# A hybrid decoder layer on one core: arithmetic moved off GpSimd at the start, rotary tables put behind the row factors, four accumulating DMAs a pass later, small tiles of 64 bytes

## The chip, the cores and the metric

The kernel runs on one core of a Trainium2 chip, in one launch. The metric is the device time in microseconds (us). Before the change three runs gave a median of 783.87 us (783.56 to 784.42).

The core has these engines: TensorE (PE in the profile; its weight loads are PEld), VectorE (DVE), ScalarE (ACT), GpSimd (POOL) and SyncE (SP), which only issues DMAs. Each runs its own queue of instructions in a fixed order and waits on semaphores for the others. VectorE, ScalarE and GpSimd work on SBUF; TensorE writes its results to PSUM.

## The reference

One decoder layer on 512 tokens of width 1024, in float32. In short:

```python
u = rms_norm(x, norm_mix_g)
proj = u @ w_in          # conv a and g (512 + 512), c_q (384), c_kv (256), k_rope (32), gates (2 x 1024)
z = a * sigmoid(g); z = depthwise_causal_conv(z, conv_w, width=31) + conv_b
conv_out = silu(layer_norm(z)) @ w_conv_out
mla_out  = latent_attention(c_q, c_kv, k_rope, cos, sin) @ w_mla_out     # 8 heads, causal
h = x + (sigmoid(g0) * conv_out + sigmoid(g1) * mla_out) @ w_out
h = h + memory_cross_attention(rms_norm(h, norm_xattn_g), rms_norm(mem, norm_mem_g))   # 4 heads, 256 memory tokens
h = h + square(relu(rms_norm(h, norm_mlp_g) @ w_mlp1)) @ w_mlp2          # 4096 wide
y = rms_norm(h, final_norm_g)
```

## The kernel before

Every product of two float32 matrices is done with three matmuls on rounded halves: a matrix is split into hi (a cast to the matmul type on ScalarE, L202) and lo (a subtract, L203, on VectorE or GpSimd), and `mm3` (L237 to L239) adds hi·hi, hi·lo and lo·hi into one PSUM bank. The weights come in chunks of 1 MB from HBM into two `raw` buffers through SyncE's queue. `prep` splits a chunk's part into one of three `wh`/`wl` pairs, and `w_eng[0]` says which engine does the subtract. `Pipe` splits one unit ahead of the matmuls that use it.

The order of TensorE's instructions is the program's. `after(ticks, fn)` puts a small piece of work some steps of `mm3` later into that order. The queues of the other engines are ordered by a scheduler when the program is built: it takes what is ready first by its own model of time, and of several ready ones the one that comes first in the program. On the chip that order is fixed.

The first stage (L608 to L641) computes the projection onto the conv channels, in four channel tiles of an a and a g half each. For channel tile 0 the transfers of `x` and of the weights still arrive; per block of 128 rows of `x`, `split_x` makes `uh` and `ul` (L206, L207), and the weight block is split, its lo part on GpSimd from block 1 on. `x_stats` squares x and adds up the eight squares, three adds on VectorE and four on GpSimd (L579, L580). For channel tile 1 the weights' lo is made on VectorE, from channel tile 2 on by GpSimd. After the a half of tile 1 `x_rows` sums the squares over the rows with eight small matmuls (L277) and computes the row factors `rx` on VectorE (L279, L245 to L250), then `rx2`, its square (L584). Five steps later `x_bcast` transposes `rx` (L271), copies it to `rbx` and evacuates the g half of tile 0 with it (`evac_g`, L600 to L605); then it makes the tables of the rotary angles (`rope_tables`, L439 to L462: four multiplies at L444, one per token tile, and some twenty steps on 128x64), which depend on constants and positions alone. The sines themselves are ScalarE's (L467, L468). The conv taps (L492, L494: 31 per channel tile on VectorE) begin as soon as a tile's gate is ready, and are spread over the projections that follow.

The memory branch keeps its row factors in `rm`, 2 values per row, in the pool `xm`; the pools `mg` (`mgh`, `mgl`: the merged branches) and `x2` are stacked on it. `xm` also holds the split memory (`mh`, `ml`), its keys and its values (`xvh`, `xvl`).

The last stage is the second MLP matrix in seven passes over sums of blocks (`PASSES`, L1384; four units `c` each), which replaces eight products of blocks by seven. Its weight operands are sums of the four blocks b11, b12, b21 and b22. They are formed in place: `add_to` (L1356) issues a DMA from GpSimd that adds a block of `w_mlp2` from HBM to a tile in SBUF. The tiles `xs[c]` start as b11 (`load_x`, SyncE's queue). Each of the passes 0, 2 and 4 reads `xs[c]` and then adds the next block, for the pass two later; pass 3 does the same with `vs[c]`. Pass 1 reads `b21[c]`, loaded in passes 0 and 1 by `load_b21` into tiles that other blocks have left; `load_v` loads b22 in pass 2. Two of the blocks of the hidden layer (s3, a22) are spilled to HBM and read back by `reload` from ScalarE's queue.

Of the kernel before, what the change touches and what calls it, by code (L numbers as in the profile page):

```python
# [14 lines left out]
F32 = mybir.dt.float32  # L15
# [4 lines left out]
ALU = mybir.AluOpType  # L20
# [3 lines left out]
P = 128  # L24
# [144 lines left out]
def _body(tc, a):  # L169
# [3 lines left out]
    dve = nc.vector  # L173
    act = nc.scalar
    gps = nc.gpsimd

    def pool(name, bufs=1, side=None, space=None):
        kw = dict(name=name, bufs=bufs, reuse_waits="tile")
        if side:
            kw["side"] = side  # L180
        if space:
            kw["space"] = space
        cm = tc.tile_pool(**kw)
        return cm, cm.__enter__()
# [5 lines left out]
    cst_cm, cst = pool("cst")  # L190
# [10 lines left out]
    def split(hi, lo, src, eng=None):  # L201
        act.copy(hi, src)  # L202
        (eng or dve).tensor_tensor(lo, src, hi.bitcast(F32), op=ALU.subtract)  # L203
# [38 lines left out]
    def rsqrt(dst, v, n):  # L242
        t = sm.tile([P, n], F32, tag="rs_t", name="rs_t")
        ti = sm.tile([P, n], I32, tag="rs_i", name="rs_i")
        dve.tensor_scalar(ti, v.bitcast(I32), 1, None, op0=ALU.logical_shift_right)  # L245
        dve.tensor_scalar(dst.bitcast(I32), ti, -1, 0x5F3759DF, op0=ALU.mult, op1=ALU.add)
        for _ in range(3):
            dve.scalar_tensor_tensor(t, dst, -0.5, dst, op0=ALU.mult, op1=ALU.mult)  # L248
            dve.tensor_tensor(t, t, v, op=ALU.mult)
            dve.scalar_tensor_tensor(dst, t, 1.5, dst, op0=ALU.add, op1=ALU.mult)  # L250
# [10 lines left out]
    rx = cst.tile([P, NT], F32, name="rx")  # L261
    rx2 = cst.tile([P, NT], F32, name="rx2")
# [31 lines left out]
    raws = {}  # L294
# [37 lines left out]
    w_eng = [dve]  # L332
# [32 lines left out]
    xr = xp.tile([P, KD, S], F32, name="xr")  # L365
    nacc = xp.tile([P, S], F32, name="nacc")
# [62 lines left out]
    def split_x(k):  # L429
        split_scaled(uh[:, k, :], ul[:, k, :], xr[:, k, :], v_("norm_mix_g", k))  # L430


    n = NT * 16
# [5 lines left out]
    def rope_tables():  # L439
        dve.tensor_copy(posf, posi)  # L440
        fr = kon[:, K_FREQ:K_FREQ + n]
        for t in range(NT):
            sl = slice(16 * t, 16 * t + 16)
            dve.tensor_scalar(ang[:, sl], fr[:, sl], posf[:, t:t + 1], None, op0=ALU.mult)  # L444

        def fma(k, c):
            dve.scalar_tensor_tensor(ang, k, -c, ang, op0=ALU.mult, op1=ALU.add)

        dve.tensor_scalar(k_, ang, 1.0 / TWO_PI, MAGIC, op0=ALU.mult, op1=ALU.add)
        dve.tensor_scalar(k_, k_, MAGIC, None, op0=ALU.subtract)  # L450
        dve.tensor_scalar(kh, k_, 2.0 ** -11, MAGIC, op0=ALU.mult, op1=ALU.add)
        dve.tensor_scalar(kh, kh, MAGIC, 2048.0, op0=ALU.subtract, op1=ALU.mult)
        dve.tensor_tensor(k_, k_, kh, op=ALU.subtract)
        for c in PI_PARTS:
            fma(kh, c)
            fma(k_, c)
        dve.tensor_scalar(k_, ang, 1.0 / TWO_PI, MAGIC, op0=ALU.mult, op1=ALU.add)
        dve.tensor_scalar(k_, k_, MAGIC, None, op0=ALU.subtract)
        for c in PI_PARTS:
            fma(k_, c)  # L460
        dve.tensor_scalar(ang, ang, 3.1415925, -3.1415925, op0=ALU.min, op1=ALU.max)
        dve.scalar_tensor_tensor(k_, ang, -1.0, ang, op0=ALU.mult, op1=ALU.max)  # L462
# [109 lines left out]

    hold = {}

    def x_stats():
        for k in range(KD):
            act.activation(xr[:, k, :], xr[:, k, :], AF.Square)
            if k > 1:
                (dve, gps)[k % 2].tensor_tensor(xr[:, k % 2, :], xr[:, k % 2, :], xr[:, k, :], op=ALU.add)  # L579
        gps.tensor_tensor(nacc, xr[:, 0, :], xr[:, 1, :], op=ALU.add)  # L580

    def x_rows():
        rstd_rows(nacc, D, rx)
        dve.tensor_tensor(rx2, rx, rx, op=ALU.mult)  # L584

    def x_bcast():
        b = bcast_rows(rx)
        act.copy(rbx, b)
        hold["a"] = fa
        evac_g(fg, 0)  # L590
        act.copy(identb, ident)
        act.copy(maskb, kon[:, K_MASK:K_MASK + 128])
        rope_tables()


    def evac_a(b, c):
        hold["a"] = b
# [12 lines left out]
    for k in range(KD):  # L610
        hl = first[k // 4]
        if k == 0:
            dve.tensor_copy(hl[0][:, 0], raws[0][:, 0])
            dve.tensor_tensor(hl[1][:, 0], raws[0][:, 0], hl[0][:, 0].bitcast(F32), op=ALU.subtract)
        split_x(k)
        if k == 1 or k > 0 and k % 2 == 0:
            kn = 1 if k == 1 else 2
            sl = slice(k % 4, k % 4 + kn)
            split(hl[0][:, sl], hl[1][:, sl], raws[0][:, k:k + kn], gps)
        for i, j in ((0, 0), (1, 0), (0, 1)):  # L620
            for b, c0 in ((fa, 0), (fg, 128)):
                pe.matmul(b, hl[i][:, k % 4, c0:c0 + 128], (uh, ul)[j][:, k, :],
                          start=k == 0 and i == j == 0, stop=k == KD - 1 and j == 1)
        tick(2.0)
# [10 lines left out]
        evac_g(b, 1)  # L635

    for c in range(1, CT):
        w_eng[0] = dve if c == 1 else gps
        proj_unit(("ag", c), 0, evac_a1 if c == 1 else lambda b, c=c: evac_a(b, c))
        proj_unit(("ag", c), 128, evac_g1 if c == 1 else lambda b, c=c: evac_g(b, c))  # L640
    pipe.flush()  # L641
# [195 lines left out]
    for t in range(NT):  # L837
        b = bank()
        sl = slice(t * P, (t + 1) * P)
# [56 lines left out]
    xm_cm, xmp = pool("xm", side="right")  # L896
# [4 lines left out]
    mh = xmp.tile([P, KD, MEM], F32R, name="mh")  # L901
    ml = xmp.tile([P, KD, MEM], F32R, name="ml")
    rbm = xmp.tile([P, MEM], F32, name="rbm")
    rm = xmp.tile([P, 2], F32, name="rm")
    mg_cm, mgp = pool("mg", side="right")
    mgh = mgp.tile([P, KD, S], F32R, name="mgh")
    mgl = mgp.tile([P, KD, S], F32R, name="mgl")
# [32 lines left out]
    def mem_norm():  # L940
        ms = sm.tile([P, 2], F32, tag="mss", name="mss", bufs=1)
        for t in range(2):
            act.activation(mtok[:, t, :], mtok[:, t, :], AF.Square, accum_out=ms[:, t:t + 1])
        v = sm.tile([P, 2], F32, tag="rv2", name="rv2", bufs=1)
        dve.tensor_scalar(v, ms, 1.0 / D, EPS, op0=ALU.mult, op1=ALU.add)
        rsqrt(rm, v, 2)
        for k in range(KD):
            split_scaled(mh[:, k, :], ml[:, k, :], mr[:, k, :], v_("norm_mem_g", k))
        after(D_M, mem_bcast)
# [260 lines left out]
    xs, vs = {}, {}  # L1210
# [145 lines left out]
    def add_to(t, what, c):  # L1356
        gps.dma_start(out=t, in_=hbm(what, c), accum_op=ALU.add, max_dma_last_dim=8192)  # L1357

    def w_source(n, c):

        if n in (0, 2, 4, 6):
            return xs[c], {0: "b12", 2: "b22", 4: "b21"}.get(n)
        if n in (3, 5):
            return vs[c], {3: "b12"}.get(n)
        return b21[c], None

    b21 = {}
# [94 lines left out]
    def pass_unit(n, c):  # L1462
        aname, bk, again = PASSES[n]
        end = n == len(PASSES) - 1

        def prep_():
            if aname in SPILLED:
                for cc in {0: (0, 1), 3: ()}.get(c, (c + 1,)):
                    reload(aname, cc)
            src, nxt = w_source(n, c)  # L1470
            h, w = split_h(aname, c), split_w(v3(src))
            if n == 0 and c >= 2:
                load_b21(c - 2)
            if n == 1 and c < 2:
                load_b21(2 + c)
            if n == 2:
                load_v(c)
            if nxt:
                add_to(src, nxt, c)
            return h, w  # L1480

        def main(hw):
            h, w = hw
            if c == 0 and not again:
                acc_[bk] = [bank("at" if bk in "bd" else "mm") for _ in range(2)]
            if end and c == 2:
                held["hw"] = hw
            elif end and c == 3:
                for t in range(2):
                    part(acc_[bk][t], t, *held["hw"], False, False, again)  # L1490
                    part(acc_[bk][t], t, h, w, False, True, again)
                    DONE[n](t)
            elif c in (0, 3):
                for t in range(2):
                    part(acc_[bk][t], t, h, w, c == 0 and not again, c == 3, again)
                    if c == 3:
                        DONE[n](t)
            else:
                chunk(acc_[bk], h, w, c, again)
            if n == 0 and c == 0:  # L1500
                late_pools()
                load_x(3)
            if n == 2 and c == 0:
                m2w["gf"] = w_tile(m2w["p"], "b21", "gf")[:, :D]
                dma(out=m2w["gf"], in_=a["gfin"].to_broadcast([P, D]))
        pipe.unit(prep_, main)
# [32 lines left out]
```

## Time and profile before

| what | value |
|---|---|
| median of 3 runs | 783.87 us |
| profiled execution, its time | 785.28 us |
| its span, first to last instruction | 783.5 us |
| mean granted clock of TensorE | 0.991 |
| PE busy | 757.7 us (97%), 3594 matmuls |
| PEld busy | 626.3 us (80%) |
| DVE busy | 526.9 us (67%) |
| ACT busy | 400.3 us (51%) |
| POOL busy | 91.2 us (12%), 70 instructions |
| DMA | 103.36 MB, 132 GB/s over the span |

Busy time is the time in which an engine has an instruction at work; matmuls overlap their neighbours, so the mean of one (389 ns) is longer than the time from one start to the next. [...] In lists in order of time the number in brackets is the engine's idle time ahead of the row, and behind the arrow stands what ended it. "POOLq", "SPq" and "ACTq" are the queues that issue DMAs.

### The profile page before, as it was taken

What the parts mean: (1) busy time and instruction counts of PE and PEld (TensorE: products, weight loads), DVE (VectorE), ACT (ScalarE), POOL (GpSimd) and SP (SyncE); (2) the same over time, 40 slices, a digit from 0 to 9 for tenths busy, and PEclk for the clock granted to TensorE, in tenths of its full rate; (3) what the DMA queues carried; (4) which work ended last, traced back from release to release, by engine and by line L of the source; (5) the groups of instructions that cost most, each with busy time, mean ns of one, the idle gap of its engine ahead of it and who ended that gap; (6) DMA issues with size and microseconds to landing.
All of it is one profiled execution on the core that took longest, in us unless ns stands there. A gap on an engine that the chain in (4) does not pass through costs nothing.

```text
span 783.5 us, 9480 instructions
## 1 busy us (share of the span) xinstructions
PE 757.7 (97%) x3594; PEld 626.3 (80%) x3594; DVE 526.9 (67%) x845; ACT 400.3 (51%) x681; POOL 91.2 (12%) x70
## 2 busy tenths in 40 slices
PE   8799999999999999999999999999999979999996
PEld 4589789778788887889888888888888868888784
DVE  5898999944788869756687634333333546767995
ACT  7422244378766647434474644444444445665662
POOL 4434436330000000000000000000000000111000
PEclk9899999999999999999999999999999999999998
DMA  8313223312203134424231424334253696999731
GB/s 277 106 40 108 84 85 108 107 54 95 94 1 108 55 108 161 161 63 154 108 108 54 162 92 164 135 132 179 106 215 109 184 277 239 246 231 214 192 108 54
DMA packets 26990, 103.36 MB, mean 132 GB/s; under 512 B 2369, under 2 KB 9921, under 8 KB 17985
## 3 DMA queue, kind: packets, MB, share of 16 engines
q1 hardware_dynamic: 13600, 67.54, 24.1%
q0 software_dynamic: 2304, 16.78, 10.5%
q10 hardware_dynamic: 11040, 18.45, 6.8%
q8 instruction: 28, 0.46, 0.3%
q14 instruction: 18, 0.14, 0.1%
HBM read 94.37 MB, written 8.39 MB: 131 GB/s over the span
## 4 chain that ended last, share of the span: by engine, by line
PE 79%; DVE 13%; DMA 3%; ACT 2%; issue 2%; SPq 0%; DVEq 0%; ACTq 0%
PE mm L239 20%; PE mm L237 20%; PE mm L238 20%; DVE cv L494 6%; PE at L238 4%; PE at L239 4%; PE at L237 4%; DMA a<-weights 2%; PE at L812 1%; PE at L793 1%; DVE wl L203 1%; DMA xr<-xT 1%; DVE rs_t L248 1%; DVE sg L721 1%; PE at L794 1%
## 5 line engine op out<-in xcount | busy, mean ns | idle before, releaser
L202 ACT CAST wh<-raw 128x1024 fp32r<-128x1024 f32 (+4 forms) x103 | 102.6, 998 | 193.0 <-PE mm L238 165.5
L203 DVE TENSOR_TENSOR wl<-raw,wh 128x1024 fp32r<-128x1024 f32 (+1 forms) x71 | 85.7, 1207 | 105.7 <-ACT wh L202 105.5
L237 PE MATMUL mm<-hgh,wh 128*128 128x512 f32 x288 | 113.2, 393 | 0.0
L238 PE MATMUL mm<-hgl,wh 128*128 128x512 f32 x288 | 112.2, 389 | 0.0
L239 PE MATMUL mm<-hgh,wl 128*128 128x512 f32 x288 | 112.2, 389 | 0.0
L494 DVE SCALAR_TENSOR_TENSOR cv<-zpad,vec,cv 128x512 f32<-128x512 f32 x116 | 80.0, 743 | 0.1
L203 POOL TENSOR_TENSOR wl<-raw,wh 128x1024 fp32r<-128x1024 f32 (+4 forms) x32 | 66.1, 2066 | 96.7 <-ACT wh L202 96.7
L237 PE MATMUL mm<-uh,wh 128*128 128x512 f32 x176 | 71.0, 404 | 2.3 <-DVE sg L721 2.1
L1357 POOL DMA_DIRECT2D x<-weights x12 | 10.5, 879 | 516.1 <-DVE wl L203 496.1
L239 PE MATMUL mm<-uh,wl 128*128 128x512 f32 x176 | 69.7, 396 | 0.5 <-DVE wl L203 0.5
L238 PE MATMUL mm<-ul,wh 128*128 128x512 f32 x176 | 69.6, 395 | 0.0
L239 PEld LDWEIGHTS mm<-hgh,wl 128*128 128x128 f32 x288 | 54.1, 188 | 11.4
L237 PEld LDWEIGHTS mm<-hgh,wh 128*128 128x128 f32 x288 | 54.1, 188 | 10.9
L238 PEld LDWEIGHTS mm<-hgl,wh 128*128 128x128 f32 x288 | 54.1, 188 | 10.9
L203 DVE TENSOR_TENSOR wl<-x,wh 128x1024 fp32r<-128x1024 f32 x25 | 30.3, 1220 | 18.9 <-ACT wh L202 18.9
L237 PEld LDWEIGHTS mm<-uh,wh 128*128 128x128 f32 x176 | 33.8, 192 | 10.7 <-issue 4.2
L239 PEld LDWEIGHTS mm<-uh,wl 128*128 128x128 f32 x176 | 33.6, 191 | 8.3 <-DVE wl L203 1.0
L238 PEld LDWEIGHTS mm<-ul,wh 128*128 128x128 f32 x176 | 33.7, 192 | 6.6
L202 ACT CAST wh<-x 128x1024 fp32r<-128x1024 f32 x25 | 26.2, 1051 | 24.4 <-PE at L239 9.7
L238 PE MATMUL at<-wl,hA 128*128 128x512 f32 x96 | 37.6, 391 | 0.6 <-DVE wl L203 0.6
L239 PE MATMUL at<-wh,hB 128*128 128x512 f32 x96 | 37.4, 389 | 0.0
L237 PE MATMUL at<-wh,hA 128*128 128x512 f32 x96 | 37.4, 389 | 0.0
(392 smaller groups left out, 1721.2 us busy)
## 6 DMA issues: line engine op xcount, KB each, us to landing
raw<-weights SPq DMA_DIRECT2D x42, 1024.0 KB, 4.9
x<-weights POOLq DMA_DIRECT2D x12, 1024.0 KB, 11.6
a<-weights SPq DMA_DIRECT2D x5, 1024.0 KB, 9.1
x<-weights SPq DMA_DIRECT2D x4, 1024.0 KB, 6.0
raw<-weights SPq DMA_DIRECT2D x4, 768.0 KB, 4.3
xr<-xT SPq DMA_DIRECT2D x8, 256.0 KB, 6.1
raw<-weights SPq DMA_DIRECT2D x4, 512.0 KB, 5.0
ht<-xT ACTq DMA_DIRECT2D x1, 2048.0 KB, 9.1
```

The source lines that it names most:

```text
L202: act.copy(hi, src)
L203: (eng or dve).tensor_tensor(lo, src, hi.bitcast(F32), op=ALU.subtract)
L237: pe.matmul(out, wh, ah, start=first and i == 0, stop=False, **kw)
L238: pe.matmul(out, wh, al, start=False, stop=False, **kw)
L239: pe.matmul(out, wl, ah, start=False, stop=last and i == n - 1, **kw)
L248: dve.scalar_tensor_tensor(t, dst, -0.5, dst, op0=ALU.mult, op1=ALU.mult)
L494: dve.scalar_tensor_tensor(run if w < CW - 1 else acc[:, c, :], zs, wcol, run, op0=ALU.mult, op1=ALU.add)
L721: dve.tensor_tensor(t, b, rbx, op=ALU.mult)
L793: pe.matmul(b[:, :n], q[:, 0, sl], k[:, 1, :n], start=False, stop=False)
L794: pe.matmul(b[:, :n], q[:, 1, sl], k[:, 0, :n], start=False, stop=True)
L812: pe.transpose(b[:, (t - k) * P:(t - k + 1) * P], ptok[h, t][:, k * P:(k + 1) * P], ident)
L1357: gps.dma_start(out=t, in_=hbm(what, c), accum_op=ALU.add, max_dma_last_dim=8192)
```

## The change

Five edits:

- The lo part of channel tile 0's weights, the adds of `x_stats` and the lo parts of channel tile 2's weights are done by VectorE. From channel tile 3 on GpSimd does them as before.
- VectorE's instructions of `rope_tables` are queued behind the one that writes `rx2`. `tc.issue_after(ins)` orders what its block issues on the engine of `ins` behind `ins`; it adds no wait.
- The four DMAs that add b12 to `xs[c]` are issued in pass 1 instead of pass 0, each behind a copy on GpSimd (`pace`) of one column of the first lo weights of pass 1's unit c. Pass 2 reads the sums, as before.
- `rm` has 16 columns (64 bytes in each partition) instead of 2.
- The new tile `paced` has 16 columns as well, in the pool of constants at the left.

```diff
+    rx_done = []
     def x_stats():
         for k in range(KD):
             act.activation(xr[:, k, :], xr[:, k, :], AF.Square)
             if k > 1:
-                (dve, gps)[k % 2].tensor_tensor(xr[:, k % 2, :], xr[:, k % 2, :], xr[:, k, :], op=ALU.add)
-        gps.tensor_tensor(nacc, xr[:, 0, :], xr[:, 1, :], op=ALU.add)
+                dve.tensor_tensor(xr[:, k % 2, :], xr[:, k % 2, :], xr[:, k, :], op=ALU.add)
+        dve.tensor_tensor(nacc, xr[:, 0, :], xr[:, 1, :], op=ALU.add)
     def x_rows():
         rstd_rows(nacc, D, rx)
-        dve.tensor_tensor(rx2, rx, rx, op=ALU.mult)
+        rx_done.append(dve.tensor_tensor(rx2, rx, rx, op=ALU.mult).ins)
...
-        rope_tables()
+        with tc.issue_after(rx_done[0]):
+            rope_tables()
...
-            split(hl[0][:, sl], hl[1][:, sl], raws[0][:, k:k + kn], gps)
+            split(hl[0][:, sl], hl[1][:, sl], raws[0][:, k:k + kn])
...
-        w_eng[0] = dve if c == 1 else gps
+        w_eng[0] = dve if c < 3 else gps
...
-    rm = xmp.tile([P, 2], F32, name="rm")
+    rm = xmp.tile([P, 16], F32, name="rm")
...
-        rsqrt(rm, v, 2)
+        rsqrt(rm[:, :2], v, 2)
...
+    paced = cst.tile([P, 16], F32, name="paced")
+    def pace(lo):
+        return gps.tensor_copy(paced[:, 0:1], lo[:, 0, 0:1].bitcast(F32)).ins
     def w_source(n, c):
         if n in (0, 2, 4, 6):
-            return xs[c], {0: "b12", 2: "b22", 4: "b21"}.get(n)
+            return xs[c], {2: "b22", 4: "b21"}.get(n)
...
             if nxt:
                 add_to(src, nxt, c)
+            if n == 1:
+                with tc.issue_after(pace(w[0][1])):
+                    add_to(xs[c], "b12", c)
```

## Rows read from the trace of the kernel before

**Rows 1.** Order of time, TensorE: start, duration, line, tiles; last, idle time and releaser
```profile
26.23 0.95 PE L277 MATMUL at<-ones,nacc 128*128 128x1 f32 x8
...
35.64 1.09 PE L271 MATMUL at<-kon,rx 128*128 128x128 f32 x4 [4.89 <-issue]
...
41.22 0.63 PE L239 MATMUL mm<-uh,wl 128*128 128x512 f32 x1
...
645.16 0.50 PE L237 MATMUL mm<-wh,hA 128*128 128x512 f32 x1 [4.33 <-ACT s L1389]
...
743.09 0.50 PE L238 MATMUL at<-wl,hA 128*128 128x512 f32 x1 [0.61 <-DVE wl L203]
```

**Rows 2.** Order of time, VectorE, first 70 us
```profile
13.43 5.84 DVE L207 SCALAR_TENSOR_TENSOR ul<-xr,vec,uh 128x512 fp32r<-128x512 f32 x4
...
19.20 0.68 DVE L579 TENSOR_TENSOR xr<-xr 128x512 f32<-128x512 f32 x1
19.80 1.21 DVE L203 TENSOR_TENSOR wl<-raw,wh 128x1024 fp32r<-128x1024 f32 x1
...
25.06 4.88 DVE L444 TENSOR_SCALAR ang<-kon,posf 128x16 f32<-128x16 f32 x4
29.98 0.20 DVE L449 TENSOR_SCALAR k__164<-ang 128x64 f32<-128x64 f32 x1
...
32.93 0.15 DVE L279 TENSOR_SCALAR rv<-at 128x4 f32<-128x4 f32 x1
...
68.66 1.90 DVE L603 TENSOR_TENSOR sg<-sg,rbx 128x512 f32<-128x512 f32 x1 [3.17 <-ACT sg L602]
```

**Rows 3.** Order of time, GpSimd: two subtracts, and one of the accumulating DMAs
```profile
24.96 4.82 POOL L203 TENSOR_TENSOR wl<-raw,wh 128x1024 fp32r<-128x1024 f32 x2
...
630.53 0.88 POOL L1357 DMA_DIRECT2D x<-weights  x1 [1.66 <-DVE wl L203]
```

**Rows 4.** By tile, TensorE: count, ns minimum/median/maximum, first and last start, shape
```profile
L238 PE MATMUL mm<-mgl,wh x64: 395/396/504, 308.6 to 353.4; 128*128 128x512 f32 x64
...
L238 PE MATMUL mm<-hgl,wh x288: 387/389/398, 366.4 to 615.4; 128*128 128x512 f32 x144
...
L238 PE MATMUL mm<-ul,wh x176: 387/389/628, 20.1 to 191.4; 128*128 128x512 f32 x176
...
L237 PE MATMUL at<-wh,hA x96: 388/389/395, 687.7 to 773.9; 128*128 128x512 f32 x96
```

**Rows 5.** Stretches: busy us of PE, PEld, DVE, ACT, POOL, clock, DMA share, GB/s
```profile
30.00:42.00 12.00, 7.11 (x22) 5.47 (x21) 7.10 (x35) 3.78 (x7) 0.00 (x0) 0.72 0.18 66
68.00:146.00 78.00, 75.61 (x392) 65.58 (x390) 77.34 (x124) 27.91 (x53) 36.53 (x25) 1.00 0.28 97
640.80:650.00 9.20, 4.87 (x15) 3.86 (x15) 4.81 (x4) 4.89 (x6) 0.00 (x0) 0.81 1.00 282
654.00:666.00 12.00, 12.00 (x55) 9.93 (x54) 7.61 (x8) 6.46 (x8) 0.86 (x1) 1.00 0.47 162
666.00:733.00 67.00, 67.00 (x297) 55.49 (x296) 48.23 (x46) 40.39 (x45) 9.53 (x11) 1.00 1.02 229
```

**Rows 6.** Chain of waits in order of time, 620 to 650: start, us, what
```profile
629.06 13.47 DMA a<-weights
```

**Rows 7.** DMA issues, us to landing: windows 600 to 612, 629.5 to 636, 727 to 730
```profile
x<-weights SPq DMA_DIRECT2D x1, 1024.0 KB, 5.0
...
x<-weights POOLq DMA_DIRECT2D x1, 1024.0 KB, 21.4
...
re_s<-s ACTq DMA_DIRECT2D x1, 512.0 KB, 7.6
```

**Rows 8.** Page, part 3, queues: packets, MB, share of 16 engines over the span
```profile
q1 hardware_dynamic: 13600, 67.54, 24.1%
q0 software_dynamic: 2304, 16.78, 10.5%
```

**Rows 9.** Order of time, ScalarE: the cast of the reloaded block
```profile
736.62 1.06 ACT L202 CAST hA<-re_s 128x1024 fp32r<-128x1024 f32 x1 [0.23 <-PE at L238]
```

## The prediction

> **What bounds the kernel now.** I read the busy shares first, then TensorE in order of time at its two long gaps, then what VectorE, GpSimd and the transfers did before each. TensorE is busy 757.7 of 783.5 us. What can be won lies in its 25.8 idle us, in the slow clock behind the gaps, and in matmuls that take longer than others.
>
> First gap: TensorE stands 4.89 us until the transposes of L271 at 35.64 [rows 1]. They need rx, so VectorE is late: its row factors start at 32.93 only [rows 2], though the sums that they read (L277) were through at 27.2 [rows 1]. In between stand the rotary tables, and these were slow: four multiplies of 128x16 took 4.88 us while GpSimd ran two subtracts, 24.96 to 29.78 [rows 2, 3]; the next table step, 128x64, took 0.20. [...]
>
> From 68 to 146 VectorE is busy 77.34 of 78 us, TensorE 75.61 [rows 5]: both nearly full. VectorE's last slack before that is 3.17 us ahead of L603 at 68.66, where it waits for ScalarE [rows 2].
>
> Second gap: 4.33 us before 645.16, clock 0.81 in the 9.2 us from 640.8 [rows 1, 5]. The chain of waits names a load of b21 of 13.47 us [rows 6]; the same size took 5.0 us while no accumulating DMA was out [rows 7]. The four of pass 0 are: the last is issued at 630.53 and lands 21.4 us later, near 652 [rows 3, 7].
>
> **The change, part by part.** The sum is made against the profiled execution (span 783.5, time 785.28: 1.78 us lie outside the span). The median of the runs, 783.87, is 1.41 below it.
>
> *GpSimd's work to VectorE.* VectorE takes over a subtract of 128x256 (some 0.4, from the 0.68 of a 512-wide add), three of 128x512 (0.68), four adds (three squares and nacc, 0.68) and the two subtracts of channel tile 2 (1.21): 0.4 + 2.0 + 2.7 + 2.4 = 7.5 us [rows 2]. Given back: four L207 took 5.84 from 13.43, at 0.68 they are 2.7, so 3.1 less; the four table multiplies at 0.20 are 0.8 for 4.88, so 4.1 less [rows 2]. Net 0.3 more: VectorE is about as full as before, but the 3.1 come off the first 20 us, where TensorE waits for ul. Bounds there: 0 (x's transfers set the pace) and 3.1. I take 1.5, the middle: neither row is nearer.
>
> *Tables behind the row factors.* Only VectorE's order changes. With TensorE 1.5 us earlier the sums are through at 25.7. The factors are twelve small steps; between 32.93 and 35.6, with table steps among them, they took 2.7. One 1.21 us subtract may stand in front. So rx is there by 29.6, and L271 comes up at 30.75 - 1.5 = 29.25. I drop the 0.35: the 4.89 us go, and with the gap its slow clock, 6.0 us of work at half rate (35.64 to 41.6), 3.0 lost. Together 7.9; bounds 5 (1.21 us more in front, slow clock half kept) and 7.9. What is late next: the tables, some 27 steps of 0.2, 5.4 us, now run from 29.5 among the first gate evacuations, and the conv taps of L494 queue behind both, perhaps 2 us less ahead than TensorE. The 3.17 us at 68.66 cover that, because the wait there hangs through ScalarE on TensorE [rows 2]; without this cover each us is paid in full in the stretch to 146. The two sines on ScalarE wait for the tables, and nothing waits for them before the key rotation, some 100 us on. Front: 1.5 + 7.9 = 9.4.
>
> *Small tiles of 64 bytes.* In the layout a tile of 8 bytes takes 32. So rm puts its pool and those stacked on it (xkh, mh, xvh, mgh and their halves) 32 bytes off the place within 64 bytes that all other large tiles share. The matmuls show a difference: median 396 ns with mgl against 389 with hgl, ul and hA, all 512 wide [rows 4]. 192 matmuls with mgh or mgl, 48 with mh or ml, 24 with xvh or xvl: 264 x 7 ns = 1.8 us, TensorE being full there. Bounds 0 and 1.8; I take 1.8, since three neighbours agree on 389. The tile paced, 64 bytes, moves everything on the left by 64, which keeps that place; rival C doubts it. [...]
>
> *Accumulating DMAs one pass on.* Nothing is then beside the load of b21 at 629.06, so it takes 5.0 instead of 13.47 [rows 6, 7] and lands near 634, before its cast is due at some 638. The 4.33 go, and the slow clock: 0.19 x 2 x 9.2 = 3.5 us at half rate, of which some 3.2 with work, 1.6 lost. Together 5.9. Each moved step issues a one-column copy on GpSimd (0.20, the small VectorE step, or three times that) and the DMA (0.88 [rows 3]). The copy waits for the first wl of its unit in pass 1. Behind it on GpSimd stand only the next such steps, and no engine waits for GpSimd there. SP's loads (b21, v, gf) have their own queue and share only the DMA engines. Due times, an estimate from the pace of the units, 24 matmuls at 67 us for 297, so 5.4 us [rows 5]: issue near 633.5, 639.5, 644.5, 648.5; pass 2 reads the four tiles some 18 to 20 us later. Landing: 5.0 for such bytes alone, 21.4 at worst [rows 7]; issued 5 us apart instead of 2.5, I take 12 to 15: in time.
>
> Given back: the sixteen accumulating DMAs cost 10.5% of 783.5, 82.3 us of all engines, 5.1 each; a plain MB costs 2.8 (24.1% for 67.54 MB) [rows 8]. From 666 to 733 the engines are full at 1.02 [rows 5]. In the place that pass 0's four leave (20.6 us) some 5 MB of other transfers fit, 14 us; so 6.5 us of engine time are lost there. Free later on are 12 x 0.53 = 6.4, between 654 and 666 [rows 5]. So the sixteenth lands when it did, within 1 us. Behind it comes the reload of s3's third block: it took 7.6 us and was cast at 736.62, for the unit whose second matmul starts at 743.09 [rows 1, 7, 9]. Of these 6.5 us the cast is 1.06 and the matmul ahead some 1, so 4.4 are slack. TensorE wants the reload 5.9 earlier, it comes 1 earlier: 4.9 - 4.4 = 0.5 us late. Bounds 0 and 5.9. Net 5.4.
>
> Sum: 9.4 + 1.8 + 5.4 = 16.6. Span 766.9, that execution 768.7, median **767.3 us**.
>
> **The rivals.**
> A. *VectorE becomes the bound of the first 68 us.* The 7.5 us come without the relief (if it was not GpSimd that slowed those steps). Less 3.17 of slack, 4.3 are lost: 771.6. For it: VectorE is full up to 146. Against: the multiplies end just as GpSimd does, and the next step takes 0.20 [rows 2, 3].
> B. *The wait only moves.* The DMA engines stay the bound, and the reload of pass 5, or pass 2's tiles, come late by what was won: 5.4 lost, 772.7. For it: 67 us at 1.02, landings of 21.4. Against: the 6.4 free us ahead of pass 2. [...]
> C. *Slower.* What costs the 7 ns is the place not in 64 bytes but in 128, and paced moves every left tile, wh and wl among them, off the good one. Then the wide matmuls pay: 288 + 176 + 96 on each of three lines [rows 4] are 1680, and 750 of the page's other matmuls (3594 in all) lie on the same weights: 2430 x 7 ns = 17.0, and the 1.8 are not won: 786.1. It decides from 2340 on. For it: no large tile of before lies at the new place. Against: 7 ns are about 16 of the 512 columns that pass in 226 ns, 64 bytes.
> D. *The tables do not let go.* Splits stand ahead of the factors, and half of the 4.89 stays, without the slow clock: 769.8.
>
> **How the numbers follow.** Forecast 0.60, A 0.14, B 0.13, C 0.05, D 0.05, no net effect 0.03. The forecast's own ends: 1.6 more in the first 20 us and some 2 of the 2.4 idle us of 68 to 146 [rows 5] saved besides give 763.5; 2.9 less at the tables gives 770.2. A, B and D reach to 772.7; with a us on each side 763 to 774. Faster by over 0.2% (1.6 us, about what a measurement tells from none): forecast, A, B and D, 0.92. Within it 0.03. Slower, C, 0.05.
>
> **What would show it.** Right: no gap over 1 us before L271, clock 1.00 from 25 to 45 and from 630 to 650; table multiplies near 0.2 us, L207 below 0.8; mgl at 389 ns; the b21 load under 7 us; pass 1's DMAs landing within 16. Wrong: TensorE waiting for VectorE between 30 and 68 (A), for re_s or for x in pass 2 (B), 396 ns with hgl (C), rx still behind splits (D).

## The result and the profile after

The changed kernel takes 774.56 us, median of four runs (774.36 to 775.09), against 784.14 of the kernel before beside them: ratio 0.988 (95% interval 0.986 to 0.990). The forecast was 767.3 with a range of 763 to 774, so the direction was right, the gain of 16.6 us came out at 9.6 to 10.2, and the time lies half a us above the range. The profiled execution took 775.09 us, span 773.2.

I matched the matmuls of both traces one by one in program order and read how far TensorE runs ahead of the kernel before (times of before in brackets): 9.4 us at the end of the first projection (41.7), 7.1 at 262, 7.1 at 640, 13.2 at 665, 12.4 at 742, 10.6 at 745, 10.4 at the end. Two steps up, as forecast; between them two slow slides and one step down.

The front. In order of time on TensorE, in the changed kernel, the row sums, the transposes that had waited 4.89 us [rows 1], and a matmul late in pass 5:

```profile
24.54 0.95 PE L277 MATMUL at<-ones,nacc 128*128 128x1 f32 x8
...
28.98 0.62 PE L271 MATMUL at<-kon,rx 128*128 128x128 f32 x4
...
732.50 0.50 PE L238 MATMUL at<-wl,hA 128*128 128x512 f32 x1 [2.42 <-DVE wl L203]
```

L271 has no idle time ahead of it now. The last row had 0.61 before [rows 1] and has 2.42. VectorE in order of time:

```profile
15.51 1.41 DVE L207 SCALAR_TENSOR_TENSOR ul<-xr,vec,uh 128x512 fp32r<-128x512 f32 x2
...
25.53 0.16 DVE L279 TENSOR_SCALAR rv<-at 128x4 f32<-128x4 f32 x1 [2.19 <-PE at L277]
...
26.41 1.22 DVE L203 TENSOR_TENSOR wl<-raw,wh 128x1024 fp32r<-128x1024 f32 x1
...
28.91 0.16 DVE L586 TENSOR_TENSOR rx<-rx 128x4 f32<-128x4 f32 x1
...
29.19 0.65 DVE L444 TENSOR_SCALAR ang<-kon,posf 128x16 f32<-128x16 f32 x4
```

Two of L207 take 1.41 us where four took 5.84, four of L444 take 0.65 where they took 4.88 [rows 2], and the row factors run from 25.53 to 29.07 with one subtract of 1.22 among them.

The stretches of [rows 5] in the changed kernel (same columns; its own times):

```profile
30.00:42.00 12.00, 12.00 (x53) 9.64 (x52) 11.86 (x26) 4.64 (x6) 4.43 (x2) 1.00 0.07 30
...
640.80:650.00 9.20, 9.20 (x42) 7.55 (x41) 6.05 (x6) 5.05 (x5) 1.07 (x2) 1.00 1.04 252
654.00:666.00 12.00, 12.00 (x54) 9.87 (x53) 9.06 (x9) 7.67 (x9) 1.72 (x2) 1.00 1.03 275
```

The granted clock, a share of TensorE's full speed, is 1.00 where it was 0.72 and 0.81, TensorE has no idle time there, and the transfer engines are full from 654 to 666, where before they had half of the time free.

The slide. Two stretches that hold the same 1122 matmuls, first the kernel before, then the changed one:

```profile
42.00:266.00 224.00, 219.83 (x1122) 185.39 (x1121) 187.66 (x339) 117.89 (x231) 59.03 (x35) 1.00 0.23 78
```

```profile
32.56:258.90 226.34, 223.07 (x1122) 185.35 (x1121) 191.91 (x351) 120.81 (x236) 58.99 (x35) 1.00 0.22 77
```

2.34 us longer, and TensorE does not stand more (3.3 us idle against 4.2): it is busy 3.2 us longer with the same work. By tile, TensorE, as in [rows 4]:

```profile
L238 PE MATMUL mm<-mgl,wh x64: 387/393/506, 301.6 to 346.3; 128*128 128x512 f32 x64
...
L238 PE MATMUL mm<-hgl,wh x288: 387/389/397, 359.3 to 608.4; 128*128 128x512 f32 x144
...
L238 PE MATMUL mm<-ul,wh x176: 388/394/399, 18.8 to 183.6; 128*128 128x512 f32 x176
...
L237 PE MATMUL at<-wh,hA x96: 388/392/398, 674.7 to 763.5; 128*128 128x512 f32 x96
```

`ul` went from 389 to 394 ns and `hA` from 389 to 392, `hgl` stayed, and `mgl` came from 396 to 393 only. From start to start the medians are 227 ns where nothing is lost and 233 for `uh` and `ul`.

The step down. The chain of waits of the changed kernel in pass 5 (start, us, what):

```profile
713.18 1.06 ACT hA L202
714.25 1.24 DVE hB L203
715.51 11.30 DMA re_s<-s
726.89 1.06 ACT hA L202
727.98 1.23 DVE hB L203
...
730.57 0.74 DVE y L1406
731.31 1.15 DVE wl L203
732.50 0.50 PE at L238
```

The reload of s3's third block can be issued only when VectorE has made the lo half of the first one (they share a buffer), and takes 11.30 us instead of 7.6 [rows 7].

### The profile page after: what moved, and what is told of

Its sections match the earlier page's. It is cut to its first block, busy times and chain, and to the rows that moved or that the text cites. A ratio compares the mean times of both kernels' runs of the same rounds, so it can differ in the third digit from the quotient of the medians.

```text
span 773.2 us, 9487 instructions
## 1 busy us (share of the span) xinstructions
PE 756.4 (98%) x3594; PEld 623.8 (81%) x3594; DVE 525.3 (68%) x855; ACT 399.9 (52%) x681; POOL 76.4 (10%) x64
## 4 chain that ended last, share of the span: by engine, by line
PE 80%; DVE 13%; DMA 3%; ACT 2%; issue 1%; SPq 0%; DVEq 0%; ACTq 0%
PE mm L239 21%; PE mm L238 21%; PE mm L237 21%; DVE cv L494 6%; PE at L238 4%; PE at L237 3%; PE at L239 3%; DMA re_s<-s 1%; PE at L816 1%; DVE wl L203 1%; PE at L797 1%; DVE rs_t L248 1%; DMA xr<-xT 1%; PE at L798 1%; PE at L795 1%
## 5 line engine op out<-in xcount | busy, mean ns | idle before, releaser
L203 DVE TENSOR_TENSOR wl<-raw,wh 128x1024 fp32r<-128x1024 f32 (+3 forms) x77 | 90.7, 1178 | 106.7 <-ACT wh L202 106.4
L494 DVE SCALAR_TENSOR_TENSOR cv<-zpad,vec,cv 128x512 f32<-128x512 f32 x116 | 80.4, 744 | 0.1
L203 POOL TENSOR_TENSOR wl<-raw,wh 128x1024 fp32r<-128x1024 f32 (+2 forms) x26 | 56.4, 2169 | 107.7 <-ACT wh L202 102.9
L237 PEld LDWEIGHTS mm<-hgh,wh 128*128 128x128 f32 x288 | 54.1, 188 | 10.9
L238 PEld LDWEIGHTS mm<-hgl,wh 128*128 128x128 f32 x288 | 54.1, 188 | 10.9
L1368 POOL COPY paced<-wl 128x1 f32<-128x1 f32 x4 | 2.5, 615 | 468.2 <-DVE wl L203 468.2
```

The costliest lines, as they stand in the source:

```text
L237: pe.matmul(out, wh, ah, start=first and i == 0, stop=False, **kw)
L238: pe.matmul(out, wh, al, start=False, stop=False, **kw)
L494: dve.scalar_tensor_tensor(run if w < CW - 1 else acc[:, c, :], zs, wcol, run, op0=ALU.mult, op1=ALU.add)
L1368: return gps.tensor_copy(paced[:, 0:1], lo[:, 0, 0:1].bitcast(F32)).ins
```

## Experiments

Two theories stood at the start. *Places*: what sets a matmul's cadence is where its two operands lie against each other, and `paced` moved one of them. *Traffic*: the matmuls are slower because of what VectorE or the transfers do beside them.

**left_back.** `paced` is gone; rm stays at 64 bytes.

```diff
-    paced = cst.tile([P, 16], F32, name="paced")
-        return gps.tensor_copy(paced[:, 0:1], lo[:, 0, 0:1].bitcast(F32)).ins
+        return gps.tensor_copy(posi[:, 0:1].bitcast(F32), lo[:, 0, 0:1].bitcast(F32)).ins
```

> The changed kernel without the tile paced: the copy of one column goes into posi, a tile of constants that nobody reads by then, so that wh, wl and all other left tiles lie where they lay before the change. rm keeps its 64 bytes. Theory 1 (the place of the stationary tile against the moving one sets the cadence): matmuls of uh and ul with wh go from 233 back to 227 ns from start to start, those of hA from 229 to 232 back to 227, cq, ck and pt likewise; TensorE's lead on the kernel before stays near 9.4 us up to 266 us instead of falling to 7.1. 3.2 us less than the changed kernel's 774.6: 771.4. mgh and mgl stay slow (232 or more), since they lie at another place than wh. Rival (the cadence comes from other traffic, say VectorE's larger share of the splits or the later DMAs): uh stays at 233 and the time at 774.6 +- 0.6.

Measured: 771.84 (771.06 to 772.68), ratio 0.983 (0.982 to 0.985) to before's 784.84. By tile:

```profile
L238 PE MATMUL mm<-ul,wh x176: 387/389/397, 19.2 to 182.3; 128*128 128x512 f32 x176
...
L238 PE MATMUL mm<-mgl,wh x64: 392/394/505, 299.5 to 344.5; 128*128 128x512 f32 x64
```

`ul` is back at 389, the lead stays at 9.1 up to 262 and at 16.2 through the passes, and `mgl` is still slow. 64 bytes among the constants cost some 3 us.

**all_same.** The same, with the tiles on rm's pool at wh's place too.

```diff
-    rm = xmp.tile([P, 16], F32, name="rm")
+    rm = xmp.tile([P, 128], F32, name="rm")
```

> As left_back, and rm has 128 columns (512 bytes), so that the tiles stacked on its pool (mh, xvh, mgh and their halves) lie at the same place within 512 bytes as wh and uh. Theory 1: 227 ns with mgh and mgl too; 264 matmuls by 5 to 7 ns are 1.3 to 1.8 us less than left_back, 769.9 (769.4 to 770.4). Rival: the same as left_back and the changed kernel; or, if 232 to 235 ns with mgl come from what else happens at that stage and not from the place, left_back's time with uh at 227 and mgl at 232.

Measured: 771.33 (770.11 to 773.03), ratio 0.983 (0.981 to 0.984).

```profile
L238 PE MATMUL mm<-mgl,wh x64: 389/389/504, 298.7 to 342.6; 128*128 128x512 f32 x64
```

`mgl` is at 389, and the stretch from 262 to 355 gives 1.0 us. The median lies 1.4 above the 769.9 that was expected; it is only 0.5 better than left_back's and the ranges overlap. In the stage behind, where `mh`'s matmuls are 256 columns wide, all_same runs about 0.6 us behind left_back (120 ns from start to start against 113; there the two operands lie at the same place modulo 256 bytes in all_same and 192 apart in left_back). Why 256 columns behave otherwise was not followed.

**shift_alone.** The kernel before with the 64 bytes alone.

```diff
+    paced = cst.tile([P, 16], F32, name="paced")
+    gps.memset(paced, 0.0)
```

> The kernel before with nothing but the tile paced, 64 bytes among the left constants, and one memset that writes it. Theory 1: uh and ul with wh go from 227 to 233, hA from 227 to 229 to 232, hgh stays at 227, since hgh and wh move together; about 3 us slower than before, 787.2 (786.5 to 788). Rival (other traffic): 784.1 +- 0.5, uh at 227. The rival of the prediction in its full size, 7 ns on some 2400 matmuls, would be 801.

Measured: 788.00 (787.53 to 789.95), ratio 1.0044 (1.0029 to 1.0058): 3.4 us slower by the ratio, for a tile that nothing reads.

```profile
L238 PE MATMUL mm<-ul,wh x176: 388/394/628, 20.6 to 193.0; 128*128 128x512 f32 x176
...
L237 PE MATMUL at<-wh,hA x96: 388/397/398, 690.9 to 778.5; 128*128 128x512 f32 x96
```

**shift_256.** As shift_alone, with `[P, 64]`, 256 bytes.

> As shift_alone, with the tile paced of 64 columns, 256 bytes, instead of 16. Theory 1 (the cadence depends on the difference of the two operands' addresses modulo 256 bytes): uh, ul and hA back at 227 ns, mgl at 235 as before, time as before, 784.7 +- 0.6. [...]

Measured: 784.73 (783.22 to 786.14) beside 784.66, ratio 1.0002 (0.9991 to 1.0013).

```profile
L238 PE MATMUL mm<-ul,wh x176: 387/389/628, 20.5 to 190.3; 128*128 128x512 f32 x176
```

**places.** The cadence by itself.

```diff
+        b, g = go(0, 32)   # stationary 0, moving 32 bytes off; one such pair of lines per place
+        for s, m, f, l in g: pe.matmul(b, s, m, start=f, stop=l)
```

> It leaves out the whole computation: 68 groups of 24 matmuls of 512 columns, each group on its own line, with the stationary operand 0, 96 or 224 bytes off a place and the moving one 0 to 480 bytes off it in steps of 32; then eight places again while ScalarE and VectorE run splits of 128x1024, and again while loads of 1 MB arrive. Theory 1: a group has 227 ns from start to start where both places are the same, and some 230 to 236 where they differ, in the quiet part already; which differences cost tells the modulus (64, 128, 256 or 512 bytes). Rival: 227 in every quiet group; if the place matters only beside other engines, the second or third part shows it, and if it never does, what slowed uh was not the place.

Measured in one run, groups by line (last but one number: mean ns of one). The moving operand is 32 (L207), 128 (L213), 64 (L209), 256 (L221) and 0 bytes (L205) past the stationary one; L283 has both at 224:

```profile
L207 PE MATMUL bk<-mv,st 128*128 128x512 f32 x24 | 5.8, 395 | 0.0
...
L213 PE MATMUL bk<-mv,st 128*128 128x512 f32 x24 | 5.8, 395 | 0.0
...
L209 PE MATMUL bk<-mv,st 128*128 128x512 f32 x24 | 5.7, 392 | 0.0
...
L221 PE MATMUL bk<-mv,st 128*128 128x512 f32 x24 | 5.6, 390 | 0.0
...
L283 PE MATMUL bk<-mv,st 128*128 128x512 f32 x24 | 5.6, 390 | 0.0
...
L205 PE MATMUL bk<-mv,st 128*128 128x512 f32 x24 | 5.6, 389 | 0.0
```

What counts there is the difference (moving minus stationary) modulo 256 bytes, over the 48 quiet groups at multiples of 32. At 0 a matmul is 389 to 390 ns, 227 from start to start; at 64 it is 391 to 392 (229); at the others it is 394 to 396 (233 to 234). Four more groups, at 4, 16, 48 and 80 bytes, have 393 to 399. It shows with no other engine at work, and the parts with splits and with loads have the same numbers (392 at 64, 390 at 256). The kernel's own pairs fit (addresses modulo 256 in the built programs: before, all of these at 224 but mgl at 192; after, wh at 32, mgl at 160, uh, ul and hA at 224): in the changed kernel `uh` and `ul` lie 192 past `wh` (233.5), `mgl` 128 past it (232), `wh` 64 past `hA` (229.0 over its three lines); in the kernel before `mgl` lay 224 past it (233.3). One thing stays open: in shift_alone `wh` lies at the same 64 past `hA` and the passes run at 233, steadily, up to pass 5; those of the changed kernel run at 229. So the same pair of places settled in two rhythms here, and what chose was not found.

**move_alone.** The kernel before with the four DMAs in pass 1, no tile moved.

```diff
-            return xs[c], {0: "b12", 2: "b22", 4: "b21"}.get(n)
+            return xs[c], {2: "b22", 4: "b21"}.get(n)
...
+            if n == 1:
+                with tc.issue_after(pace(w[0][1])):
+                    add_to(xs[c], "b12", c)
```

> The kernel before with the four accumulating DMAs moved to pass 1 and nothing else; the copy goes into posi, so that no tile changes its place. Theory 1, by the changed kernel's trace: the gap of 4.33 us and its slow clock go, 6.4 us won, and the reload of pass 5 gives back 1.9: 4.5 less, 779.9 (against 784.4, the middle of the runs of before so far). The prediction's own step: 5.4 less, 779.0. Rival (the reload is late only because the kernel ahead of it became faster by other edits): 6.4 less, 778.0.

Measured: 781.23 (779.33 to 784.62, ten runs), ratio 0.996 (0.994 to 0.998): 2 to 4.5 us less. The median is 1.3 above the 779.9 of theory 1, and the runs spread over 5 us. Its trace has the step of 6 us up and

```profile
738.71 0.50 PE L238 MATMUL at<-wl,hA 128*128 128x512 f32 x1 [2.35 <-DVE wl L203]
```

so the late reload belongs to this edit and needs no other; by its trace the net is 4.4, as theory 1 has it.

**no_adds.** all_same without the four DMAs, b12 left out.

```diff
-                with tc.issue_after(pace(w[0][1])):
-                    add_to(xs[c], "b12", c)
+                pace(w[0][1])
```

> As all_same, without the four accumulating DMAs of pass 1 (the copy that paces them stays): b12 is left out of the sums of pass 2. Theory 1 (what the moved DMAs give back is transfer time: the later DMAs and the reload queue behind them): no gap over 0.5 us in pass 5, the reload of s3's third block lands within 8 us instead of 11.3, the sixteenth DMA lands at least 10 us earlier; 768.7. Rival (the reload's lateness has to do with its buffer alone): gap and landing as in all_same, 771.3.

Measured: 769.43, one run. The reload lands in 7.9 us, and

```profile
727.21 0.50 PE L238 MATMUL at<-wl,hA 128*128 128x512 f32 x1 [0.62 <-DVE wl L203]
```

The gap is back at before's size, a little over the 0.5 that was expected. The last accumulating DMA lands at 718.8, in all_same at 723.7: 4.9 earlier, half of the 10 I wrote. What the moved DMAs give back is transfer time, some 70 us later.

**third_buffer.** all_same with a third buffer for s3's blocks.

```diff
-        t = mlp.tile([P, 4, HT], F32, tag="sp_" + name, name="re_" + name, bufs=2)
+        t = mlp.tile([P, 4, HT], F32, tag="sp_" + name, name="re_" + name, bufs=3 if name == "s3" else 2)
```

> As all_same, and the blocks of s3 have three buffers instead of two, so that the reload of the third block need not wait until VectorE has made the lo half of the first. Theory 1 (the reload is late because it is issued late into a full queue: issued 715.5 in the changed kernel, 11.3 us to landing, cast 726.9): it is issued some 6 us earlier, lands before its cast is due, and the gap of 2.4 to 2.6 us at the last rows of pass 5 is under 0.5: some 2.3 less than all_same's 771.3, 769. Rival (the transfer engines are full, so it lands no earlier, or another transfer lands later by as much): the gap stays over 1.5 there or moves to the next reload, 771.3 +- 0.5.

Measured: 767.86 (767.18 to 769.46), ratio 0.979 (0.978 to 0.981). The third block's reload is issued in pass 0,

```profile
616.60 0.44 ACTq L1200 DMA_DIRECT2D re_s<-s  x1
```

some 95 us earlier and not six; the fourth, at 710.82, still takes 11.3 us and has time for it. No gap over 0.25 us is left in the passes, and the time is 1.1 under what was expected. In the passes of this kernel the full transfer engines cost nothing by themselves: they cost through a load that two buffers allow only late.

**tables_alone.** The kernel before with this edit:

```diff
+        with tc.issue_after(rx_done[0]):
+            rope_tables()
```

> The kernel before with the rotary tables queued behind rx's row factors and nothing else; GpSimd keeps its arithmetic. Theory 1 (VectorE's small steps are slow beside GpSimd's subtracts, and the tables stood ahead of the factors): the factors now come first but beside the subtracts (to 29.8 us), so rx is there by about 30 to 31, the gap of 4.89 us shrinks to under 0.8 and most of the slow clock goes: 5 to 7.9 less, 776.5 to 779.4. Rival (what holds rx back is GpSimd's part of the sums and of the splits, not the order): the gap stays over 2 us and the time within 3 of before.

Measured: 780.43 (779.37 to 780.78), ratio 0.995 (0.993 to 0.996): 4.2 less, one us short of what was expected. TensorE's gap, and VectorE and GpSimd ahead of it:

```profile
31.76 0.40 PE L271 MATMUL at<-kon,rx 128*128 128x128 f32 x2 [1.12 <-issue]
```

```profile
27.11 0.16 DVE L279 TENSOR_SCALAR rv<-at 128x4 f32<-128x4 f32 x1 [3.31 <-PE at L277]
27.31 2.37 DVE L245 TENSOR_SCALAR rs_i<-rv 128x4 int32<-128x4 int32 x1
29.71 0.17 DVE L246 TENSOR_SCALAR rx<-rs_i 128x4 int32<-128x4 int32 x1
```

```profile
24.91 4.75 POOL L203 TENSOR_TENSOR wl<-raw,wh 128x1024 fp32r<-128x1024 f32 x2
```

A step on 128x4 takes 2.37 us and ends at 29.68, with GpSimd's second subtract (29.66); the next takes 0.17. The lead is 5.8 at 41.7 and falls to 5.0 at the pass gap, where in the kernel before the chain of waits names a load of 13.47 us [rows 6]: that is the missing us.

**pool_alone.** The kernel before with GpSimd's arithmetic moved, the tables left where they were.

```diff
-                (dve, gps)[k % 2].tensor_tensor(xr[:, k % 2, :], xr[:, k % 2, :], xr[:, k, :], op=ALU.add)
-        gps.tensor_tensor(nacc, xr[:, 0, :], xr[:, 1, :], op=ALU.add)
+                dve.tensor_tensor(xr[:, k % 2, :], xr[:, k % 2, :], xr[:, k, :], op=ALU.add)
+        dve.tensor_tensor(nacc, xr[:, 0, :], xr[:, 1, :], op=ALU.add)
...
-            split(hl[0][:, sl], hl[1][:, sl], raws[0][:, k:k + kn], gps)
+            split(hl[0][:, sl], hl[1][:, sl], raws[0][:, k:k + kn])
...
-        w_eng[0] = dve if c == 1 else gps
+        w_eng[0] = dve if c < 3 else gps
```

> The kernel before with GpSimd's arithmetic of the first channel tiles on VectorE and nothing else; the rotary tables stay ahead of the row factors. Theory 1 (what made VectorE's steps slow was GpSimd's subtracts and adds beside them): the first 20 us give 1.5, the four table multiplies take 0.8 instead of 4.9, so that rx comes 4 us earlier and the gap of 4.89 us falls under 1; 5.6 less with the slow clock kept, 8.6 without: 776.1 to 779.1 (before: 784.7). With tables_alone's 4.3 this is more than the front's 9.4 together, so that each edit would do most of the work by itself. Rival (VectorE gets 7.5 us more work and no relief, rival A of the prediction): within 2 us of before, or slower.

Measured: 776.63 (775.99 to 777.78), ratio 0.990 (0.988 to 0.992).

```profile
29.50 0.62 PE L271 MATMUL at<-kon,rx 128*128 128x128 f32 x4 [0.28 <-issue]
```

Its lead grows by 7.4 us from 26 to 41.7, with both front edits by 7.7 to 7.8 (the changed kernel, left_back, all_same): with GpSimd out of the way the order of the tables is worth some 0.3 to 0.4. Two edits that remove the same wait do not add.

**psum_rows.** third_buffer, with an operand of the latent row factors' small steps in PSUM.

```diff
+    def rsqrt_ps(dst, v, b, n):
+        t, ti, d = (b[:, o:o + n] for o in (400, 408, 416))
...
+            dve.scalar_tensor_tensor(t, d, -0.5, dst, op0=ALU.mult, op1=ALU.mult)
+            dve.tensor_tensor(t, t, v, op=ALU.mult)
...
-        rsqrt(r, v, NT)
-        dve.tensor_tensor(r, r, rx, op=ALU.mult)
+        d = rsqrt_ps(r, v, bs[0], NT)
+        dve.tensor_tensor(r, d, rx, op=ALU.mult)
```

> As third_buffer, and the small steps of the latent row factors (128x4, L245 to L250 where latent_rows calls them) keep one of their operands in free columns of a PSUM bank, so that no step reads two SBUF tensors, or reads and writes SBUF with one input; three steps of 0.15 more per call. Theory (a VectorE step with two SBUF inputs, or of one input from SBUF to SBUF, stands until GpSimd's instruction has ended, one with an input in PSUM does not): the five steps that took 1.9 to 2.2 us between 72 and 135 take 0.15 to 0.25, VectorE is some 9 us less busy there, the three gaps of TensorE at 81.5, 88.4 and 136.5 (0.90, 1.21, 0.90) close: 1.5 to 3 less than third_buffer's 767.9, 765 to 766.4. Rival (the next step in line is held in their place, or TensorE then waits for ScalarE): the gaps stay and the time is 767.9 +- 0.5.

Measured: 765.72 (763.64 to 767.48), ratio 0.976 (0.974 to 0.978), the fastest of all. The stretch from 68 to 146, third_buffer first:

```profile
68.00:146.00 78.00, 75.00 (x376) 63.59 (x375) 77.71 (x129) 28.36 (x53) 35.85 (x25) 1.00 0.27 97
```

```profile
68.00:146.00 78.00, 78.00 (x395) 67.06 (x395) 71.12 (x139) 31.18 (x57) 37.10 (x26) 1.00 0.27 97
```

VectorE is 6.6 us less busy with ten more instructions, and TensorE's 3.0 idle us are gone. Not all of it reaches the end: in the profiled executions, the slowest of psum_rows (767.48) and the fastest of third_buffer (767.18), no difference is left. In that of psum_rows the granted clock is 0.69 from 192 to 196 (1.00 in third_buffer), and from 146 to 262 the lead falls by 1.5 us; and TensorE, earlier now, waits again at the pass gap, where third_buffer has no wait:

```profile
629.81 0.50 PE L237 MATMUL mm<-wh,hA 128*128 128x512 f32 x1 [1.31 <-ACT s L1412]
```

So the gain from 68 to 146 is shown; that of 2.1 us in the medians rests on four runs each, whose ranges overlap a little. Single steps of third_buffer, then of psum_rows, each beside a subtract of GpSimd:

```profile
76.15 2.39 POOL L203 TENSOR_TENSOR wl<-raw,wh 128x1024 fp32r<-128x1024 f32 x1 [2.39 <-ACT wh L202]
76.33 2.23 DVE L246 TENSOR_SCALAR rr<-rs_i 128x4 int32<-128x4 int32 x1
```

```profile
76.71 2.40 POOL L203 TENSOR_TENSOR wl<-raw,wh 128x1024 fp32r<-128x1024 f32 x1 [2.39 <-ACT wh L202]
76.88 0.14 DVE L257 TENSOR_SCALAR rr<-at 128x4 int32<-128x4 int32 x1
```

## Why the prediction was right and where it failed

Against the profiled executions 16.6 us were forecast and 10.2 came.

- *Front, 9.4 forecast, 9.4 measured.* Its parts hold as well: 1.4 in the first 20 us, the gap, and the slow clock behind it. That the first came so near is luck: 1.5 was the middle of a range of 0 to 3.1, and the traces of the other runs with this edit have 0.8 to 2.0 there. The cause is as argued: of the four table multiplies two took 2.31 and 2.38 us, each ending within 0.03 of a subtract of GpSimd, and now all four take 0.23. Rivals A and D fell: VectorE is busy 11.86 of 12 us from 30 to 42 and TensorE does not wait. The half rate that the forecast counts behind both gaps is in the trace of before: a granted clock of 0.50 from 36 to 41 us and from 646 to 649, with matmuls of 0.63 us until about 41.6 against the usual 0.39 [rows 1, 4]; in the changed kernel the clock is 1.00 from 25 to 45 and from 630 to 650. One table step (L447, 128x64) still stands 2.11 us, from 33.17, beside GpSimd's next subtract, but behind the row factors, where no matmul waits for it. Of the two edits the first does nearly all (pool_alone).
- *Pass gap, 5.9 forecast, 6.0 measured* (lead 7.1 at 640, 13.2 at 665), clock 1.00. The four moved DMAs land in 10.9, 12.7, 14.0 and 16.9 us, the last a little over the 16 named, and pass 2 waits for none. The load of b21 took 7.6 where 5.0 was forecast and under 7 was the sign of being right; the pass did not wait for it.
- *Reload of pass 5, 0.5 forecast, 1.8 measured.* This step failed in one term, "so 4.4 are slack". The prediction put the sixteenth DMA where it was, within 1 us, and the reload 1 us earlier; counted from the same lead of 7.1, they came 0.9 and 1.8 earlier. But between the cast and the matmul I counted only the cast and a matmul. The chain shows more: the lo half on VectorE (1.23), the factors and two wide steps of `finish` (L1406), then the split of wl (1.15), 5.6 us in all where before had 6.5. So the slack was 0.9 there and 0.9 ahead of the cast (landing 735.7, cast 736.62). TensorE wanted the reload 5.3 earlier (lead 12.4 at 742): 5.3 - 1.8 - 1.8 = 1.7. no_adds and third_buffer each take the gap away. Rival B's mechanism was there at a third of its size.
- *Small tiles, 1.8 forecast; nothing won and 3.1 lost.* The step that failed: "The tile paced, 64 bytes, moves everything on the left by 64, which keeps that place". The place is not one within 64 bytes that all tiles share; it is the difference between the two operands of a matmul, modulo 256 (227 to 234 ns in places; 389 for `ul` with 256 bytes in between, 394 with 64, in shift_256 and shift_alone). In the kernel before the large tiles of the left and the right had difference 0, but for those of rm's pool and the pools stacked on it; mgl lay 224 past wh. The change put every left tile at another difference to every right one (uh, ul, the latent tiles, pt, hA), 2.3 us from 42 to 266 (of which left_back, without paced, still loses 0.3) and 0.8 in the passes, and moved mgl from one bad difference to another. The size was off too: with every tile at one place (all_same) TensorE gains 1.0 us on the kernel before from 262 to 355, and nothing from there to 411. By an estimate from the starts, the 48 matmuls with mh or ml win some 0.3 there (227 to 229 ns against 233 to 235), and 96 others, with rows of 256 columns (120 against 117), which the sum left out, lose as much. Pairs on one side (hgh, oh and xoh with wh) moved together and lost nothing, which is why rival C, right in its mechanism, was far too dear at 2430 matmuls; it was weighed by how many columns pass in 7 ns, which says nothing on the modulus. The rows of before could not tell the two readings apart: 396 ns appeared there only where a shifted tile met an unshifted one. The prediction took one of them as settled.

These add up: 1.3 more at the reload, 1.8 not won and 3.1 lost are 6.2 of the 6.4 us missing.

That the places alone slow a matmul rests on the run places, 227 to 234 ns with no other engine at work; why they do is not shown. What stood beside VectorE's slow steps the traces show: a 128x4 step took 2.37 us and ended with GpSimd's subtract (tables_alone), the conv taps (L494, whose running sum is in PSUM) took 0.74 both beside the same subtracts and without them (third_buffer), and the small step took 0.14 once an operand of it was in PSUM (psum_rows).

## What to carry to other kernels

Before a tile is added or resized, write down the addresses of both operands of each large matmul modulo 256 bytes, before and after; where they were equal, a tile of 64 bytes in between cost each matmul of ul 5 ns here (389 to 394, shift_alone), other distances up to 7 of 227 ns, 3% (places), and a pad of 256 bytes cost nothing (shift_256), all with 512 columns. For 256 columns, measure. When a transfer is moved out of a gap, follow the full transfer engines to the last load that is issued late, and measure its slack along the whole chain to TensorE, the other engine's queue included; here one more buffer took the wait away while the transfer engines stayed full.

## What was not expected of the hardware

- In places, two operands of a matmul at different addresses modulo 256 bytes cost 2 to 7 ns on 227 (512 columns of float32r, multiples of 32 bytes), without any other engine at work; the same pair of places ran at 229 in one kernel and 233 in another, steadily.
- Rows of 256 columns behaved otherwise: 113 ns from start to start at a difference of 192 (left_back), 117 at 224 (before), 120 at 0 (all_same).
- VectorE steps from SBUF to SBUF on 4, 16 or 64 columns that started just behind a GpSimd subtract of 128x1024 lasted until that had ended, 2.0 to 2.4 us (third_buffer and tables_alone, before, after); with an operand in PSUM one took 0.14 (psum_rows). Five such steps cost TensorE 3 us between 68 and 146 (third_buffer against psum_rows).
